# Seven inner products in place of one product, twice, in the second input phase of a pooling trunk; two operand sums stored instead of formed again; another form of the last rows' factor

## The chip, the core and the metric

The kernel runs on one core of a Trainium2 chip. The metric is the time of one execution in device microseconds (us). Before the change three runs gave 906.63, 906.72 and 906.90 us; the median is 906.72 us.

## The reference

One layer is computed (`DEPTH = 1`, so mixer 0 alone): a pooling mixer between two norms, over 4096 frames of 1024 channels.

```python
def trailing_mean(u, window):
    seq = u.shape[1]
    cs = jnp.cumsum(u.astype(jnp.float32), axis=1)
    lagged = jnp.pad(cs, ((0, 0), (window, 0), (0, 0)))[:, :seq]
    count = jnp.minimum(jnp.arange(1, seq + 1), window).astype(jnp.float32)
    return ((cs - lagged) / count[None, :, None]).astype(u.dtype)

def pool_mixer(h, in_w, group_w, group_b, scale, out_w):
    b, s, _ = h.shape
    u, gate = jnp.split(h @ in_w, 2, axis=-1)
    ug = u.reshape(b, s, POOL_GROUPS, POOL_GROUP_DIM)
    pooled = jnp.stack([trailing_mean(ug[:, :, g], w) for g, w in enumerate(POOL_WINDOWS)],
                       axis=2) - ug
    mixed = jnp.einsum('bsgc,gcd->bsgd', pooled, group_w) + group_b
    y = mixed.reshape(b, s, POOL_WIDTH) * scale * jax.nn.silu(gate)
    return y @ out_w

def reference(...):
    h = x
    h = h + pool_mixer(rms_norm(h, norm_w[0]), ...)
    return rms_norm(h, final_norm_w)
```

## The kernel before

**Products.** Every large matrix product is cut once into halves and done as seven products of the half size, in the form of Strassen and Winograd (P1 to P7, with sums S1 to S4 of the left operand's quarters and T1 to T4 of the right one's). Each fp32 operand is split into a high part (a copy, on ACT) and a low part (a subtraction, on DVE), both of type fp32r, and a product is three passes: high by high, high by low, low by high.

**Phases.** The list `steps` has 112 products: input phase a (four blocks of 1024 frames, seven products each; the weights with the group map folded in), input phase b (the same four blocks, the other half of the outputs), and the output phase o (eight blocks of 512 frames, seven products each). In phase b the order inside a block is P1, P2, P6, P7, P5, P4, P3. A product of phase a or b (`product_in`, line 711) is 48 matmuls of 512 columns: two halves of the inner dimension, four PSUM banks, two slices, three passes. Four of the output phase's products in a block are plain, too; P2 and P4 of most blocks are themselves done as seven inner products of a quarter of the size (`mm_inner`, line 826), of 6 matmuls with 256 columns each.

**PSUM.** There are eight banks. In the input phases banks 69 to 72 (by the names in the order below) are the set x, which P1, P2, P7 and P4 write, and 73 to 76 the set y, which P6, P5 and P3 write. After P1, its result is copied from x to y so that the others add to it. A product's result is taken out by `evict_in`: after P4 four DVE additions of one bank each, then a Silu on ACT over two tiles; after P3 four ACT copies. P1 of the next block starts on x straight behind P3, bank by bank.

**Operands.** Four tiles op_85 to op_88 hold two products' token operands (two tiles each). While a product runs, `split_halves` splits the next one's operand (`split`, line 216: ACT copy, then DVE subtraction), as soon as PE has released the tile. The operands of phase b are loaded from `sd`, where phase a stores them (`split_in`, line 656; the store is put on the ACT queue, on POOL's for block 0). S1 is formed anew in phase b by `form_in` at P5 (two DVE additions for a block), S4 by `form_s4` (two subtractions) in blocks 0 and 1; blocks 2 and 3 load a stored S4.

**What sets the order.** The loop at the end of the kernel runs step n: loads for steps ahead (`load_reach`), the operand two steps ahead (`form`), the split one step ahead, the pooling work that is due (`pool_due`), then the product and its eviction. `pool` (line 891) takes the results of P4 and P3, with running sums (`TENSOR_TENSOR_SCAN`), and stores rows for phase o; for phase b it also forms sums of them (`inner_sums`) and stores these to `sumd`. `make_wo` in steps b1 P5 and b2 P5 (b1 is block 1 of phase b) loads four tiles of the output weights, scales them on ACT, combines them on DVE and stores the results to `wod`. Engines work through their own instructions in order. Tiles come from two pools, st (11 tiles) and vt (8).

**The end.** For the last 256 rows `late_factor` (line 1163) forms 1/root by a reciprocal and one step of Newton's method, and `late_vector` applies it in two pieces of 256 columns.

Of the kernel before, what the change touches and what calls it, by code (L numbers as in the profile page):

```python
# [2 lines left out]

# [12 lines left out]
P = 128  # L16
D = 1024
# [14 lines left out]
S4_STORED = (2, 3)  # L32
# [7 lines left out]
class Slots:  # L40
# [41 lines left out]
    def retire(self):  # L82
        return self.free.popleft()[1]


@with_exitstack
def kernel(
# [51 lines left out]
    def new_st(i):  # L139
# [5 lines left out]
    vt = Slots(  # L145
        [mem.tile([P, 2 * (HIST + H)], F32, tag=f"vt{i}", name=f"vt{i}") for i in range(NV)]
    )
# [58 lines left out]
    def split(dst, src):  # L206
# [20 lines left out]
        for i in range(P1, P7 + 1)  # L227
# [4 lines left out]
            for i in (P1, P2, P7, P4, *((P3,) if b in S4_STORED else ()))  # L232
# [80 lines left out]
    def store_weights(dst, h, b11, b21, b12, b22):  # L313
        nc.sync.dma_start(out=dst[P1][h], in_=b11)
        nc.sync.dma_start(out=dst[P2][h], in_=b21)
        if P2 in firsts:
            inner_rights(P2, b21)
        for i, u in combine(b11, b21, b12, b22).items():
            nc.sync.dma_start(out=dst[i][h], in_=u)
            if i in firsts:  # L320
                inner_rights(i, u)
# [59 lines left out]
    def split_wb(i):  # L381
        for h in range(2):
# [7 lines left out]
            if i != P6:  # L390
                give(u)

    QW = H // 4

    def inner_rights(i, low):

        high = firsts.pop(i)
        more = take()
# [11 lines left out]
    firsts = {}  # L410

    def make_wo(h):
        if h:
            for i in INNER:
                firsts[i] = take()
                nc.sync.dma_start(out=firsts[i], in_=wod[i][0])
# [192 lines left out]
    def load_in(q, b, i):  # L609
# [11 lines left out]
        elif i == P3 and has_s4(q, b):  # L621
            s["12"] = load_saved(b, P3)

    def has_s4(q, b):
        return q == 1 and b in S4_STORED

    def form_in(q, b, i):
# [19 lines left out]
        elif i == P5:  # L647
# [6 lines left out]
    def split_in(q, b, i):  # L654
# [6 lines left out]
        if i == P6 and (q or b) and not has_s4(q, b):  # L661
            form_s4(b)
        if i == P2 and has_s4(q, b):
            for u in s.pop(key):
                give(u)
# [3 lines left out]
        elif i not in (P1, P2, P6) and not (i == P7 and swapped(q, b)):  # L669
            for u in s.pop(key):  # L670
                give(u)
        return t

# [30 lines left out]
    def product_in(i, t, sets, by_bank, between=None, behind=None):  # L704
# [17 lines left out]
        if between and 8 in between:  # L722
            between[8]()

# [166 lines left out]
    def pool(b, q, half, vs, sgs):  # L891
# [4 lines left out]
        for g in range(2):  # L896
# [44 lines left out]
            if win > 2:  # L941
                if first:
# [3 lines left out]
                    )  # L946
                nc.vector.scalar_tensor_tensor(
# [18 lines left out]
        if q:  # L966
            if 2 * b + 1 - half in sumd:
                inner_sums(2 * b + 1 - half, sgs)
            for sg in sgs:
                give(sg)  # L970
# [8 lines left out]
    def evict_in(b, q, i, sets):  # L979
# [26 lines left out]
        else:  # L1006
            ev["12"] = [take_v() for _ in range(2)]
            for c, u in enumerate(cells(ev["12"], HIST)):
                last = copy(halved(u), plain(ps[c]))
# [132 lines left out]
    def mean_part(ss, before):  # L1142
# [3 lines left out]
            out=ms, in0=ss, scalar1=1.0 / D, scalar2=before, op0=ALU.mult, op1=ALU.add  # L1146
# [10 lines left out]
    def early_half(half, j, n):  # L1157

        u = hs[NBO - 1][half, j][:, n]
        partial[half, j] = mean_part(square_part(halved(u)), EPS)  # L1160
        mul(u, u, fw[0][:, n])

    def late_factor(half, j, parts):
# [4 lines left out]
        tmp = column()  # L1168
        rs = column()
        behind = partial["added"]  # L1170
        scaled = column()
        nc.vector.tensor_scalar(
# [561 lines left out]
```

## Time and profile before

| | |
|---|---|
| median of three runs | 906.72 us (906.63 to 906.90) |
| profiled execution | 906.22 us, of which the span is 904.2 us |
| instructions | 11947 |
| ACT | 482.8 us busy, 53% of the span |
| POOL | 39.6 us busy, 4% |
| DMA | 200.66 MB, mean 222 GB/s |

The span is the stretch from the first to the last instruction of the profiled execution. A busy time is the time in which at least one instruction of an engine ran, and a matmul's end is modelled, so that neighbouring matmuls overlap in the record: how fast PE really goes is read from the starts of successive groups. In a group's row the second number behind the bar is the mean length of one instruction; instructions of one engine that follow each other start a little earlier than the first one's end. In square brackets stands how long an engine was idle before an instruction, and what ended that.

### The profile page before, as it was taken

The numbers are of one execution on the slowest core, as the hardware profiler recorded it, in microseconds if no ns is written. First come the engines' busy times: TensorE is split into PE (matmuls) and PEld (weight loads), VectorE is DVE, ScalarE is ACT, GpSimd is POOL, SyncE is SP. The second block draws the span as 40 slices with busy tenths as digits, with TensorE's granted clock in tenths as the row PEclk, the third lists the DMA queues.
The fourth block names the chain that finished last, engine by engine and source line by source line (L and its number), as shares of the span: only waits on it lengthen the run. The fifth ranks groups of instructions, "written<-read, shape, count | busy, mean of one in ns | idle before, by whom it ended". The sixth has DMA issues, their size and how long they took to land.

```text
span 904.2 us, 11947 instructions
## 1 busy us (share of the span) xinstructions
PE 895.7 (99%) x4446; PEld 789.8 (87%) x4446; DVE 767.4 (85%) x952; ACT 482.8 (53%) x794; POOL 39.6 (4%) x73
## 2 busy tenths in 40 slices
PE   9999999999999999999999999999999999999996
PEld 7888888888888888888888888888898998999996
DVE  5999993894998997497699499789999989889887
ACT  6979557447346555345355545654445535345354
POOL 0023102001100000000000000000001000000000
PEclk9999999999999999999999999999999999999999
DMA  9986966756866835116815776855875584584652
GB/s 349 408 318 162 347 212 209 253 187 237 324 211 233 278 117 186 47 47 220 315 69 201 288 281 222 295 181 193 278 251 196 195 308 151 176 292 148 212 186 94
DMA packets 73850, 200.66 MB, mean 222 GB/s; under 512 B 6784, under 2 KB 29696, under 8 KB 73792
## 3 DMA queue, kind: packets, MB, share of 16 engines
q1 hardware_dynamic: 66720, 176.54, 55.2%
q10 hardware_dynamic: 4752, 15.74, 4.6%
q0 software_dynamic: 2320, 7.62, 2.4%
q8 instruction: 35, 0.57, 0.3%
q14 instruction: 23, 0.19, 0.1%
HBM read 127.51 MB, written 72.36 MB: 221 GB/s over the span
## 4 chain that ended last, share of the span: by engine, by line
PE 97%; DVE 1%; DMA 0%; ACT 0%; issue 0%; DVEq 0%; ACTq 0%
PE bank L698 88%; PE bank L833 6%; PE bank L473 3%; DMA early<-in_wut 0%; DVE op L189 0%; DVE w L189 0%; DVE st L189 0%; PE bank L539 0%; ACT vt L1152 0%; DVE st L1232 0%; ACT vt L1193 0%; ACT vt L203 0%; ACT columns L1175 0%; DVE st L1204 0%; DVEq L1730 0%
## 5 line engine op out<-in xcount | busy, mean ns | idle before, releaser
L698 PE MATMUL bank<-op,w 128*128 128x512 f32 x2688 | 581.3, 379 | 0.1
L698 PEld LDWEIGHTS bank<-op,w 128*128 128x128 f32 x2688 | 507.6, 189 | 73.3 <-ACT early L203 0.6
L698 PE MATMUL bank<-w,op 128*128 128x512 f32 (+1 forms) x1068 | 232.2, 377 | 0.0
L698 PEld LDWEIGHTS bank<-w,op 128*128 128x128 f32 x1068 | 198.3, 189 | 26.9 <-issue 0.2
L189 DVE TENSOR_TENSOR op<-st,op 128x1024 fp32r<-128x1024 f32 x113 | 137.2, 1218 | 51.2 <-ACT op L203 51.0
L203 ACT ACTIVATE op<-st 128x1024 fp32r<-128x1024 f32 x113 | 118.4, 1052 | 95.1 <-PE bank L698 70.7
L203 ACT ACTIVATE op<-vt 128x1024 fp32r<-128x1024 f32 x65 | 67.6, 1052 | 48.0 <-PE bank L698 27.7
L189 DVE TENSOR_TENSOR op<-vt,op 128x1024 fp32r<-128x1024 f32 x65 | 78.6, 1215 | 7.3 <-ACT op L203 7.3
L203 ACT ACTIVATE vt<-bank 128x512 f32<-128x512 f32 x96 | 54.7, 592 | 51.4 <-PE bank L698 40.0
L203 ACT ACTIVATE bank<-bank 128x512 f32<-128x512 f32 (+1 forms) x72 | 36.5, 509 | 62.8 <-PE bank L698 32.1
L189 DVE TENSOR_TENSOR st<-st,st 128x1024 f32<-128x1024 f32 (+1 forms) x51 | 56.5, 1124 | 13.6 <-ACT st L294 9.3
L203 ACT ACTIVATE w<-st 128x1024 fp32r<-128x1024 f32 (+1 forms) x29 | 27.7, 964 | 27.0 <-PE bank L698 15.8
L1232 DVE TENSOR_TENSOR vt<-bank,vt 128x512 f32<-128x512 f32 x56 | 37.9, 680 | 3.0 <-PE bank L698 3.0
L189 DVE TENSOR_TENSOR st<-st,vt 128x1024 f32<-128x1024 f32 (+1 forms) x36 | 40.2, 1142 | 0.0
L189 DVE TENSOR_TENSOR vt<-bank,vt 128x512 f32<-128x512 f32 x50 | 33.2, 685 | 8.1 <-PE bank L698 8.1
L833 PE MATMUL bank<-w,op 128*128 128x256 f32 x288 | 39.9, 275 | 0.0
L189 DVE TENSOR_TENSOR w<-st,w 128x1024 fp32r<-128x1024 f32 (+1 forms) x29 | 31.9, 1107 | 8.8 <-ACT w L203 8.6
L833 PEld LDWEIGHTS bank<-w,op 128*128 128x128 f32 x288 | 37.8, 191 | 1.3
L925 DVE TENSOR_TENSOR_SCAN vt<-vt,bf 128x512 f32<-128x512 f32 x28 | 34.5, 1269 | 1.1 <-ACT vt L203 1.1
L1086 POOL TENSOR_SCALAR oms<-oss 128x2 f32<-128x2 f32 x14 | 7.4, 531 | 617.7 <-ACT st L1113 475.4
L203 ACT ACTIVATE st<-bank 128x512 f32<-128x512 f32 x34 | 20.0, 596 | 25.5 <-PE bank L698 18.5
L189 DVE TENSOR_TENSOR vt<-vt,vt 128x1024 f32<-128x1024 f32 (+1 forms) x28 | 32.8, 1175 | 0.5 <-DMA vt<-rd 0.5
(126 smaller groups left out, 676.1 us busy)
## 6 DMA issues: line engine op xcount, KB each, us to landing
st<-sd SPq DMA_DIRECT2D x31, 512.0 KB, 5.7
st<-in_x SPq DMA_DIRECT2D x30, 512.0 KB, 5.8
st<-in_xt SPq DMA_DIRECT2D x27, 512.0 KB, 7.8
vt<-in_x SPq DMA_DIRECT2D x27, 512.0 KB, 5.4
sd<-st ACTq DMA_DIRECT2D x25, 512.0 KB, 6.0
vt<-yd SPq DMA_DIRECT2D x18, 512.0 KB, 5.6
out<-vt SPq DMA_DIRECT2D x17, 512.0 KB, 3.2
yd<-vt SPq DMA_DIRECT2D x16, 512.0 KB, 2.8
```

Source lines behind the costliest of these rows:

```text
L189: made.append(nc.vector.tensor_tensor(out=dst, in0=a, in1=b, op=op))
L203: made.append(nc.scalar.activation(dst, src, func, **how))
L473: latest[0] = nc.tensor.matmul(ps2[kk][:, j * 256 : (j + 1) * 256], a[:, kk, 2 * j + t, :], maps if len(pairs) == 1 else woven(maps), star ...
L698: latest[0] = nc.tensor.matmul(ps, a, b, start=start and n == 0, stop=stop and n == 2, skip_group_check=True).ins
L833: latest[0] = nc.tensor.matmul(dst, a[k][x_], b[k][y_], start=start and k + n == 0, stop=k == 1 and n == 2, skip_group_check=True,).ins
L925: nc.vector.tensor_tensor_scan(s[:, j, at:end], v[:, j, at:end], v[:, j, at - win : end - win], sums_of[j] if sums_of else 0.0, ALU.add, A ...
L1086: nc.gpsimd.tensor_scalar(out=ms, in0=ss, scalar1=-0.5 / D, scalar2=-0.5 * EPS, op0=ALU.mult, op1=ALU.add)
L1232: partial["added"] = nc.vector.tensor_tensor(out=dst, in0=src, in1=dst, op=ALU.add).ins
```

## The change

`INNER_IN = (0, 1)` makes P3 of blocks b0 and b1 seven inner products (`product_inner`): each is 12 matmuls of 256 columns, 84 in all. The token side needs four more sums (`token_sums`, DVE) and four more splits of 512 columns; the weight side is prepared once, at b0 P6 (`keep_sums`). Three inner products use the banks x as working space, and partial results are copied from bank to bank on ACT. Twelve DVE additions of a quarter bank (`add_shared`) bring the shared parts into the result behind the ACT copies. Six tiles of st are lent to the new operands in b0 and b1 (three for the weights through both blocks, three for the tokens during each P3). `keep_sums` overwrites a quarter of the weights of P3, which is loaded and split again at b2 P2 for the two blocks that keep the plain P3.

`STORED` makes phase a store S1 (P5) for all four blocks and S4 (P3) for all four; phase b loads them. That is 12 more stores and 12 more loads of 512 KB, and phase b forms neither S1 nor S4. The tables of waits for `pool`, of the tiles kept free and of the reach of the loads get new values in phase b. `late_factor` replaces the Newton step, and the last `late_vector` is cut at 128 columns (pieces of 128 and 384) in place of 256. `inner_rights` loads its first tile itself, behind the stores of `make_wo`, where `make_wo` took it ahead of its own loads.

```diff
+INNER_IN = (0, 1)
+STORED = {3: (0, 1, 2, 3), 5: (0, 1, 2, 3)}
...
     def load_in(q, b, i):
...
-        elif i == P3 and has_s4(q, b):
-            s["12"] = load_saved(b, P3)
+        elif q and is_stored(i, b):
+            s["11" if i == P5 else "12"] = load_saved(b, i)
...
     def form_in(q, b, i):
...
-        elif i == P5:
+        elif i == P5 and not (q and is_stored(P5, b)):
             for h in range(2):
                 add(s["11"][h], s["2"][h], s["11"][h])
...
+    def token_sums(t, us):
+        b11, b12, b21, b22 = (
+            u.rearrange("p k (s a) -> p k s a", s=2)[:, :, :, n * P : (n + 1) * P]
+            for u in us for n in range(2)
+        )
...
+        sub(b11, b12, b11)
+        sub(b12, b22, b12)
+        sub(b22, b22, b11)
+        sub(b21, b21, b22)
...
+            split(dst, src)
...
+    def mm_inner_in(left, right, banks_, n, start):
+        a = inner_left_w[left]
+        for c in range(2):
+            for k in range(2):
+                for m, (x_, y_) in enumerate(((0, 0), (0, 1), (1, 0))):
...
+                        latest[0] = nc.tensor.matmul(
+                            quarter_bank(banks_[c], n), a[:, x_, k, c * P : (c + 1) * P],
+                            right[:, y_, k], ...)
...
+    def product_inner(t, sets):
+        r, tags = t
+        y, x = sets["y"], sets["x"]
+        in_turn[0] = None
+        mm_inner_in("A22", r["T4"], y[2:4], 0, False)
+        mm_inner_in("A11", r["B11"], x[2:4], 0, True)
+        for c in range(2):
+            copy(quarter_bank(x[c], 0), quarter_bank(x[2 + c], 0))
+        mm_inner_in("A12", r["B21"], y[0:2], 0, False)
+        mm_inner_in("S2", r["T2"], x[0:2], 0, False)
+        for c in range(2):
+            copy(quarter_bank(x[c], 1), quarter_bank(x[c], 0))
+        mm_inner_in("S4", r["B22"], y[0:2], 1, False)
+        mm_inner_in("S3", r["T3"], x[0:2], 1, False)
+        mm_inner_in("S1", r["T1"], x[2:4], 1, True)
+        for tag in tags:
+            restore(tag)
+
+    def add_shared(us, sets):
+        x = sets["x"]
...
+        for c in range(2):
+            into(c, 1, quarter_bank(x[c], 0))
+        for c in range(2):
+            for n in range(2):
+                latest_add = into(2 + c, n, quarter_bank(x[c], 1))
+        drained.append(latest_add)
+        for c in range(2):
+            into(c, 0, quarter_bank(x[2 + c], 0))
+            for m in range(2):
+                into(2 * m + c, 1, quarter_bank(x[2 + c], 1))
...
     def late_factor(half, j, parts):
...
-        partial["last"] = nc.scalar.activation(tmp, ss, AF.Sqrt, bias=before, scale=1.0 / D)
...
-        nc.vector.reciprocal(out=rs, in_=tmp)
-        nc.vector.scalar_tensor_tensor(
-            out=tmp, in0=rs, scalar=ms, in1=rs, op0=ALU.mult, op1=ALU.mult
-        )
-        nc.vector.scalar_tensor_tensor(
-            out=rs, in0=tmp, scalar=1.5, in1=rs, op0=ALU.add, op1=ALU.mult
-        )
+        partial["last"] = nc.scalar.activation(root, ss, AF.Sqrt, bias=before, scale=4.0 / D)
+        ms = mean_part(ss, before)
+        inverse = column()
+        nc.vector.reciprocal(out=inverse, in_=ms)
+        nc.vector.reciprocal(out=rs, in_=root)
+        nc.vector.scalar_tensor_tensor(
+            out=rs, in0=root, scalar=inverse, in1=rs, op0=ALU.mult, op1=ALU.add
+        )
...
-            late_vector(half, 1, n, factors[1], 2)
+            late_vector(half, 1, n, factors[1], H // 4)
...
     def pool_later(n):
-            wait = 0 if kind == "a" else 1 if b < NB - 1 else 2
+            wait = 0 if kind == "a" else (2, 1, 1, 2)[b]
...
-            wait = 1 if kind == "a" else 2 if b < NB - 1 else 5
+            wait = 1 if kind == "a" else (2, 3, 2, 5)[b]
...
-        return 3 if kind == "a" and i == P6 else 4 if kind == "o" else 3
+        return 2 if kind == "b" and b - 1 in INNER_IN and i in (P1, P2, P6) else 4 if kind == "o" else 3
...
+        if INNER_IN and kind == "b" and b == INNER_IN[0] and i == P6:
+            with tc.issue_after(latest_split[0]):
+                keep_sums(kept)
+        if INNER_IN and kind == "b" and b == INNER_IN[-1] and i == P3:
+            for tag in left_tags:
+                restore(tag)
```

Three places of the order show where the change sits. The first is PE at the end of b1. A row is a line of code, an operation, the tile it writes and the tiles it reads (stationary, for `product_in`, listed second), the columns, and how many alike follow each other. Before, P3 is eight groups of six, and P1 of b2 follows on bank_69:

```order
L698 MATMUL bank_73<-op_87,w_0_803 128x512 x6
L698 MATMUL bank_74<-op_87,w_0_803 128x512 x6
L698 MATMUL bank_75<-op_87,w_0_803 128x512 x6
L698 MATMUL bank_76<-op_87,w_0_803 128x512 x6
L698 MATMUL bank_73<-op_88,w_1_804 128x512 x6
L698 MATMUL bank_74<-op_88,w_1_804 128x512 x6
L698 MATMUL bank_75<-op_88,w_1_804 128x512 x6
L698 MATMUL bank_76<-op_88,w_1_804 128x512 x6
L698 MATMUL bank_69<-op_85,w_0_77 128x512 x6
```

And now, from the fourth group of six on (r_st are the lent tiles):

```order
L816 MATMUL bank_72<-op_87,w_0_817 128x256 x6
L816 MATMUL bank_73<-op_88,w_1_818 128x256 x6
L816 MATMUL bank_74<-op_88,w_1_818 128x256 x6
L816 MATMUL bank_69<-r_st_3431,r_st_2743 128x256 x6
L816 MATMUL bank_70<-r_st_3431,r_st_2743 128x256 x6
L816 MATMUL bank_73<-op_88,w_0_817 128x256 x6
L816 MATMUL bank_74<-op_88,w_0_817 128x256 x6
L816 MATMUL bank_69<-r_st_3434,r_st_2749 128x256 x6
L816 MATMUL bank_70<-r_st_3434,r_st_2749 128x256 x6
L816 MATMUL bank_71<-r_st_3437,r_st_2746 128x256 x6
L816 MATMUL bank_72<-r_st_3437,r_st_2746 128x256 x6
L783 MATMUL bank_69<-op_85,w_0_77 128x512 x6
```

P3 now writes banks 69 to 72, which P4 used just before and P1 of the next block needs straight behind.

The second place is DVE there, from P4's eviction on. Before, the eviction is followed by the pooling scans:

```order
L189 TENSOR_TENSOR vt_101<-bank_69,vt_101 128x512
L189 TENSOR_TENSOR vt_101<-bank_70,vt_101 128x512
L189 TENSOR_TENSOR st_90<-st_89,st_90 128x1024
L189 TENSOR_TENSOR vt_105<-bank_71,vt_105 128x512
L189 TENSOR_TENSOR vt_105<-bank_72,vt_105 128x512
L189 TENSOR_TENSOR op_86<-st_96,op_86 128x1024
L925 SCALAR_TENSOR_TENSOR vt_103<-vt_100,bf_1_2_0_3381 128x512
L925 SCALAR_TENSOR_TENSOR vt_103<-vt_100,bf_1_2_1_3384 128x512
L925 SCALAR_TENSOR_TENSOR vt_107<-vt_106,bf_1_3_0_3394 128x512
```

Now two scans stand ahead of the additions that free the banks (bf is a column that ACT computes):

```order
L215 TENSOR_TENSOR vt_106<-bank_71,vt_106 128x512
L215 TENSOR_TENSOR vt_106<-bank_72,vt_106 128x512
L215 TENSOR_TENSOR op_86<-st_95,op_86 128x1024
L1070 SCALAR_TENSOR_TENSOR vt_105<-vt_100,bf_1_2_0_3608 128x512
L1070 SCALAR_TENSOR_TENSOR vt_105<-vt_100,bf_1_2_1_3611 128x512
L215 TENSOR_TENSOR op_87<-st_92,op_87 128x1024
L848 TENSOR_TENSOR vt_101<-bank_69,vt_101 128x2x128
L848 TENSOR_TENSOR vt_103<-bank_69,vt_103 128x2x128
L848 TENSOR_TENSOR vt_101<-bank_70,vt_101 128x2x128
L848 TENSOR_TENSOR vt_103<-bank_69,vt_103 128x2x128
```

The additions on bank_69 come behind two scans and the low part of another operand, and wait for ACT's copies of P3's own banks.

The third place is DVE ahead of b2 P6, whose operand (the subtraction of two loaded tiles, then op_85) is now written into the tile that `inner_sums` has just stored:

```order
L1094 SCALAR_TENSOR_TENSOR vt_100<-vt_100,vt_102 128x2x512
L215 TENSOR_TENSOR w_0_817<-s_st_3588,w_0_817 128x2x256
L215 TENSOR_TENSOR vt_106<-vt_100,vt_106 128x1024
L215 TENSOR_TENSOR s_st_3038<-vt_107,vt_106 128x512
L215 TENSOR_TENSOR s_st_3038<-s_st_3038,vt_107 128x512
L215 TENSOR_TENSOR st_95<-vt_106,s_st_3038 128x512
L215 TENSOR_TENSOR s_st_3038<-vt_105,s_st_3589 128x1024
L215 TENSOR_TENSOR st_95<-vt_102,s_st_3590 128x1024
L215 TENSOR_TENSOR op_85<-s_st_3038,op_85 128x1024
```

Before, the same stretch read:

```order
L947 SCALAR_TENSOR_TENSOR vt_107<-vt_107,vt_106 128x2x512
L189 TENSOR_TENSOR st_95<-vt_101 128x512
L189 TENSOR_TENSOR vt_105<-vt_107,vt_105 128x1024
L189 TENSOR_TENSOR op_87<-st_99,op_87 128x1024
L189 TENSOR_TENSOR st_93<-vt_101,vt_105 128x512
L189 TENSOR_TENSOR st_93<-st_93,vt_101 128x512
L189 TENSOR_TENSOR op_88<-st_94,op_88 128x1024
L189 TENSOR_TENSOR st_95<-vt_105,st_93 128x512
L189 TENSOR_TENSOR st_93<-st_98,st_92 128x1024
L189 TENSOR_TENSOR st_96<-st_93,st_96 128x1024
L189 TENSOR_TENSOR op_85<-st_89,op_85 128x1024
```

The kind of work is the same; its place moved: behind P3's additions now, before them in the old order.

193 lines of the change are left out of this document (144 added, 49 removed).

## The prediction

> **What bounds the kernel now.** I read the page's busy times first, then its chain of waits, then PE's own waits.
>
> ```profile
> span 904.2 us, 11947 instructions
> PE 895.7 (99%) x4446; PEld 789.8 (87%) x4446; DVE 767.4 (85%) x952; ACT 482.8 (53%) x794; POOL 39.6 (4%) x73
> PE 97%; DVE 1%; DMA 0%; ACT 0%; issue 0%; DVEq 0%; ACTq 0%
> PE bank L1341 <- PEq L1719: 0.8, 1, 0.8
> PE bank L473 <- DMA early<-in_wut: 0.6, 1, 0.6
> ```
>
> PE is busy for 99% of the span and holds 97% of the chain that ended last. The last two rows are all its waits (total, times, longest): 1.4 us, both outside phase b. So an edit counts if it shortens PE's own work, makes PE wait, or sits behind the last matmul. DVE and ACT count only if they become late.
>
> Two groups of one line give phase b its place:
>
> ```profile
> L698 PE MATMUL bank<-op,w x2688: 379/379/483, 30.7 to 612.5; 128*128 128x512 f32 x192
> L698 PE MATMUL bank<-w,op x1068: 272/379/403, 612.7 to 896.9; 128*128 128x512 f32 x174, 128*128 128x256 f32 x4
> ```
>
> The first is all 56 products of both input phases (56 x 48 = 2688), the second the output phase. Phase b ends at 612.7. With no PE wait in it, it began 28 products earlier.
>
> **The price of a product.** The output phase already has both kinds of matmul behind each other; the second number of a row is its length, x12 and x6 its matmuls:
>
> ```profile
> 662.58 2.76 PE L698 MATMUL bank<-w,op 128*128 128x512 f32 x12
> 665.17 0.83 PE L833 MATMUL bank<-w,op 128*128 128x256 f32 x6
> ...
> 668.52 0.83 PE L833 MATMUL bank<-inner_T,op 128*128 128x256 f32 x6
> 669.19 1.03 PE L698 MATMUL bank<-w,op 128*128 128x512 f32 x4
> ```
>
> Ends are modelled, so I take starts. From 662.58 to 665.17, 12 matmuls of 512 columns take 2.59 us, 215.8 ns each. From 665.17 to 669.19 the six groups, 36 matmuls of 256 columns, take 4.02 us, 111.7 ns each. A plain P3 is 48 x 215.8 = 10.36 us; phase b thus starts at 612.7 - 28 x 10.36 = 322.6. Seven inner products are 84 x 111.7 = 9.38 us. Each replaced P3 saves 0.98 us of PE, and b0 and b1 together **1.96 us**. That is the ceiling of the main edit; an eighth of the columns goes (42 of 48 matmuls' worth), but the smaller matmul costs 3.8 ns more than half of the large one.
>
> A price below the row's is excluded by no row but has none for it; one above it has this:
>
> ```profile
> L833 PEld LDWEIGHTS bank<-w,op 128*128 128x128 f32 x288 | 37.8, 191 | 1.3
> ```
>
> Here 288 weight loads keep the loader busy for 37.8 us, 131 ns each, more than a matmul of 256 columns. In the rows above they are hidden all the same (111.7 ns from start to start). I take 111.7; if a load set the pace with the new operands, an inner P3 would be 84 x 131 = 11.0 us, 0.6 more than the plain one. That is rival R.
>
> The Trainium skill ("TensorE: Matmul & The Clock Gate", section "Back-to-back issue gap") speaks against the change: it gives about 81 ns for a matmul with its load at 128 columns and 131 ns at 512 in a sustained stream, so that narrow ones are dear per column. On a line between the two, my estimate is some 98 ns at 256: 8.2 us for an inner product against 6.3 for a plain one, a loss of 1.9 each, 3.8 us in all. This trace's 215.8 and 111.7 agree with neither figure, nor with their ratio.
>
> **What DVE and ACT get.** Busy time of PE, PEld, DVE and ACT (count in brackets), in blocks b0, b1 and b2 of phase b:
>
> ```profile
> 322.40:395.00 72.60, 72.60 (x338) 63.58 (x337) 53.84 (x59) 34.36 (x46) 0.00 (x0) 1.00 0.30 102
> 395.00:467.50 72.50, 72.50 (x338) 63.48 (x337) 54.33 (x54) 34.98 (x68) 0.00 (x0) 1.00 0.49 181
> 467.50:540.10 72.60, 72.60 (x338) 63.58 (x337) 56.61 (x60) 36.53 (x69) 0.00 (x0) 1.00 0.69 254
> ```
>
> DVE is idle for 18.8 us in b0 and 18.2 us in b1. Its prices, from rows of several instructions or from start to start:
>
> ```profile
> 438.08 2.35 DVE L189 TENSOR_TENSOR st<-st,st 128x1024 f32<-128x1024 f32 x2
> 454.53 1.28 DVE L189 TENSOR_TENSOR vt<-bank,vt 128x512 f32<-128x512 f32 x2
> 456.86 1.31 DVE L189 TENSOR_TENSOR vt<-bank,vt 128x512 f32<-128x512 f32 x2
> 460.25 3.63 DVE L925 TENSOR_TENSOR_SCAN vt<-vt,bf 128x512 f32<-128x512 f32 x3 [0.41 <-ACT vt L203]
> 881.63 1.42 DVE L841 TENSOR_TENSOR st<-bank,st 128x256 f32<-128x256 f32 x4 [0.98 <-PE bank L833]
> L203 ACT ACTIVATE bank<-bank 128x256 f32<-128x256 f32 x24 | 8.8, 368 | 30.7 <-PE bank L833 15.5 <-DVE vt L1232 12.2 <-DVE st L1232 3.0
> ```
>
> That is 1.14 us for 1024 columns (2.35 less the overlap of a tenth), 0.60 for 512, 0.355 for a quarter bank, 1.2 for a scan, and on ACT 0.37 for a copy from bank to bank. Removed from DVE: S1 in four blocks (8 additions) and S4 in two (4 subtractions), 12 x 1.14 = 13.7 us. Added: `keep_sums` 8 x 0.60 = 4.8; for each inner P3 four sums and four low parts, 8 x 0.60, and 12 quarter additions, 4.3, so 9.1 each and 18.2 for two; the restored quarter of the weights 0.6. That is 23.6, **net +9.9 us**, 9.3 of it in b0 and 4.5 in b1, less in the others. Both fit into the idle time, so the totals cost nothing and only the hand-overs can; without that slack PE would wait for up to 9.3 us in b0 and 4.5 in b1. On ACT a P3 adds four copies from bank to bank (1.5 us) and four high parts of 512 columns, against some 37 us idle in a block.
>
> **Hand-overs at P3.** I walk b1 with t = 0 at P4's first matmul; PE's groups by the prices above. P4 ends at 10.36, and the seven inner products follow in steps of 1.34 until P1 of b2 wants bank_69 at 19.74. The engines' side starts from these rows:
>
> ```profile
> 447.12 1.06 ACT L203 ACTIVATE op<-st 128x1024 fp32r<-128x1024 f32 x1 [4.12 <-PE bank L698]
> 457.53 1.06 ACT L203 ACTIVATE op<-st 128x1024 fp32r<-128x1024 f32 x1 [0.63 <-PE bank L698]
> ```
>
> They are the splits released by the ends of P5 and P4 (10.4 us apart, P4 from 446.95). The first new operand, T4's low part, is ready at about 6.3 and needed at 10.36. P4's last bank leaves by DVE at 11.3 (the pair at 456.86 ends at 458.17, 11.2 after 446.95) and the inner product A11 B11 needs it at 12.37. The two bank copies behind A11 B11 end at 13.3 and 14.1, needed at 14.38 and 15.05; the second pair at 16.4 and 16.9, needed at 17.06 and 17.73. The last quarter addition on bank_69 ends at 19.45, P1 needs it at 19.74. That **0.3 us** is the smallest margin. It counts on DVE having done the two scans and the low part of op_87, 3.5 us, between the eviction at 11.3 and the first addition at about 17; in b0 it is 0.65 us. A stall here is bounded by one late quarter addition behind a scan, 0.36 + 1.2 = 1.6 us, and below by nothing. I take nothing.
>
> **Hand-overs of data.** `pool` for b0's P3 now comes one product later, and on SP two of the loads of `make_wo` in b1 stand behind its two `sumd` stores. Before:
>
> ```profile
> 419.55 0.33 SPq L279 DMA_DIRECT2D st<-in_out_w  x1
> 423.89 1.33 ACT L294 ACTIVATE st<-st,colt 128x512 f32<-128x512 f32 x2 [6.31 <-DMA st<-in_out_w]
> 434.54 2.49 DVE L189 TENSOR_TENSOR st<-st,st 128x1024 f32<-128x1024 f32 x2 [4.23 <-ACT st L294]
> st<-in_xt SPq DMA_DIRECT2D x27, 512.0 KB, 7.8
> ```
>
> A load landed 4.3 us after its issue (419.55 to 423.89), then two scalings of 0.6, then DVE, which had waited 4.23 us for them. Queued behind that wait on DVE are the low parts of P3's operands and the evictions of P5. A product later, the chain ends about 1.2 us before these are due, and P3's front bears 1.5 us more: a stall comes only from 2.7 us on. A load of 7.8 us, the slowest median for 512 KB here, is 3.5 late and stalls 0.8; one whose tile also waits for a slow store stalls longer (rival C). I take nothing, since 4.3 is the landing at this very place.
>
> The operand of b2 P6 is formed in a tile that `sumd` must have left. The same wait before:
>
> ```profile
> 472.68 2.05 SPq L885 DMA_DIRECT2D sumd<-st  x2
> 475.48 2.48 DVE L189 TENSOR_TENSOR st<-st,st 128x1024 f32<-128x1024 f32 x2 [1.10 <-DMA sumd<-st]
> 477.99 1.23 DVE L189 TENSOR_TENSOR op<-st,op 128x1024 fp32r<-128x1024 f32 x1
> DMA to landing us min/median/max: 2.6/4.1/7.5
> ```
>
> The store landed 2.8 us after its issue (472.68 to 475.48). Now the operand would be ready 19.3 us into b2 and is needed at 20.9. That bears a store of 4.4 us; the slowest of all `sumd` transfers, 7.5 us, would cost 3.1. I take nothing; ends 0 and 3.1. The other added loads and stores (24 x 512 KB) pass where DMA works at 0.30 and 0.49 of its time in b0 and b1; in phase a tiles come back some us later, with 3.4 us in hand at the tightest place I found (P1 of a's b1). DMA is hidden there by the two products' lead of the splits.
>
> **The end.** The last rows' factor:
>
> ```profile
> 898.52 0.29 ACT L1175 ACTIVATE columns<-columns 128x1 f32<-128x1 f32 x1
> 898.85 0.16 DVE L1181 RECIPROCAL columns<-columns 128x1 f32<-128x1 f32 x1
> 899.04 0.22 DVE L1182 SCALAR_TENSOR_TENSOR columns<-columns 128x1 f32<-128x1 f32 x1
> 899.30 0.16 DVE L1185 SCALAR_TENSOR_TENSOR columns<-columns 128x1 f32<-128x1 f32 x1
> 899.49 0.88 DVE L1204 SCALAR_TENSOR_TENSOR st<-st,columns,st 128x256 f32<-128x256 f32 x2
> ```
>
> Root, reciprocal, two steps, product. The reciprocal of the mean fits under the root, and one step goes: 899.49 - 899.30 = **0.19 us**. The other cut of the last piece (128 and 384 columns) is the same work; its second store is half as large again, 0.1 us or so either way, which I leave out.
>
> **Sum.** The profiled execution took 906.22 us (span 904.2, 2.0 around it): 906.22 - 1.96 - 0.19 = 904.07. The median of the runs is 0.50 above that execution, so against 906.72 it is **904.6**.
>
> **Rivals.**
> A, the forecast: the whole gain, no new wait, 904.2 to 905.0 (the end's piece, and a few tenths of bank_69).
> B: one short wait takes the gain's place: bank_69 late at P1 (to 1.6 us), or the `sumd` store ahead of b2 P6 (to 3.1 us). 905.0 to 907.7. For it: margins of 0.3 and 1.6 us found by a walk with errors of their own; against it: the landings at these places, 2.8 and 4.3 us, are short.
> C, slower: `make_wo` in b1. Its third tile must be stored before it is loaded; a store of 7.5 instead of 4.1 us and a load of 7.8 instead of 4.3 make the chain 6.9 us late, 2.7 are borne, P3's front stalls 4.2 us: 908.8. It decides from 4.7 us on, where 2.0 of stall takes the gain. For it: SP's queue holds both stores ahead; against it: both slow at once, at a DMA share of 0.49.
> R: weight loads set the pace of the new matmuls: 906.72 + 2 x 0.6 - 0.19 = 907.7. Against it stand the 36 matmuls at 111.7. By the skill's two figures it would be 906.72 + 3.8 - 0.2 = 910.3, an estimate.
>
> **How the numbers follow.** A 0.56, B 0.21, C 0.20, R 0.03. A measurement of this kernel tells 0.2%, 1.8 us, from no change: faster is below 904.91, slower above 908.53. Of A a chance of 0.04 lies between 904.91 and 905.0. Faster 0.52; same 0.04 + 0.21 + 0.03 = 0.28; slower C, 0.20. The range runs from A with 0.3 more at the end and 0.4 of scatter, 903.9, over B to 908.0, and leaves out C's own value.
>
> **What would show it.** Right: in b0 and b1 the matmuls of 256 columns start 0.67 us apart in sixes, P3 lasts 9.4 us, phase b ends at 610.7 by the profile, and PE waits for nothing in it. For B, PE waits on DVE for a bank at the first matmul of b1 or b2, or on the low part of op_85 at b2 P6 with DVE idle for a `sumd` store. For C, DVE idles on ACT's scaling in b1 P5 and PE waits at P3's front. For R, sixes more than 0.7 us apart. At the end, the product after the reciprocal comes one step of 0.19 us sooner. The forecast is wrong if PE waits anywhere in phase b, phase a included, where I judged the later tiles to cost nothing.

## The result

The changed kernel takes 910.41 us (median of 6 runs, 908.79 to 911.81) against 906.55 us (906.32 to 906.90) in the same runs: a ratio of 1.0042, interval 1.0032 to 1.0052. It is 0.4% **slower**; the forecast was 904.6, and its range ended at 908.0.

The page of the profiled execution (911.81 us, the slowest of the six, of which the span is 910.0) begins:

```profile
span 910.0 us, 12205 instructions
PE 897.5 (99%) x4518; PEld 792.0 (87%) x4518; DVE 776.0 (85%) x985; ACT 489.0 (54%) x815; POOL 40.3 (4%) x77
PE 80%; DVE 11%; DMA 5%; issue 2%; ACT 1%; DVEq 0%; SPq 0%; ACTq 0%
```

PE is still busy for 99%, but of the chain that ended last it holds 80%, not 97%: 11% has gone to DVE and 5% to DMA. PE's own waits (total, times, longest):

```profile
PE bank L783 <- DVE op L215: 4.1, 2, 2.2
PE bank L1493 <- PEq L1894: 0.8, 1, 0.8
PE bank L783 <- DVE vt L848: 0.5, 1, 0.5
PE bank L497 <- DMA early<-in_wut: 0.2, 1, 0.2
PE bank L816 <- ACT bank L229: 0.2, 1, 0.2
PE bank L816 <- DVE vt L215: 0.2, 1, 0.2
```

The first row is new and the largest: two waits for the low part of an operand. The rows with L816 lie in b1's P3, the one with L848 at the first matmul behind it. The waits add up to less than the loss: a modelled matmul end reaches into each of them, and slower matmuls are no wait. So I count from start to start: the time from a product's first matmul to the next product's, for all 56 products of the input phases. Those that changed (us):

```
product        before   changed
a1 P7           10.36     10.55
a3 P1           10.36     12.88
b0 P6           10.36     14.22
b0 P3           10.36      9.38
b1 P3           10.36     11.23
b2 P1           10.36     10.46
```

The sum is +6.56 us, and the output phase begins 6.5 us later by the profile (619.2 against 612.7). From there to the end of the span it is 290.8 us against 291.5. So the inner product costs what was forecast (9.38), and three places give back far more: **the two largest, a3 P1 and b0 P6 with 6.4 us together, lie outside the products that were changed.** This is the profiled execution; the median of the runs lost 3.9 us, and how much less each place cost in the other runs is not known.

**Where DVE is late.** DVE in phase a's block 2 of the changed kernel (start, length, operation, and in brackets how long it was idle and what ended that):

```profile
221.97 1.23 DVE L215 TENSOR_TENSOR st<-st,st 128x1024 f32<-128x1024 f32 x1 [2.43 <-DMA st<-wvd]
...
230.44 1.22 DVE L215 TENSOR_TENSOR st<-vt,st 128x1024 f32<-128x1024 f32 x1 [3.94 <-DMA st<-wvd]
...
239.86 2.36 DVE L215 TENSOR_TENSOR vt<-vt,vt 128x1024 f32<-128x1024 f32 x2 [4.08 <-DMA vt<-rd]
...
249.08 1.22 DVE L215 TENSOR_TENSOR op<-vt,op 128x1024 fp32r<-128x1024 f32 x1
...
252.86 1.22 DVE L215 TENSOR_TENSOR op<-vt,op 128x1024 fp32r<-128x1024 f32 x1
```

And the same stretch before the change:

```profile
222.94 1.23 DVE L189 TENSOR_TENSOR st<-vt,st 128x1024 f32<-128x1024 f32 x1 [4.76 <-DMA st<-wvd]
...
232.34 2.36 DVE L189 TENSOR_TENSOR vt<-vt,vt 128x1024 f32<-128x1024 f32 x2 [0.46 <-DMA vt<-rd]
...
241.56 1.21 DVE L189 TENSOR_TENSOR op<-vt,op 128x1024 fp32r<-128x1024 f32 x1
...
245.34 1.22 DVE L189 TENSOR_TENSOR op<-vt,op 128x1024 fp32r<-128x1024 f32 x1
```

The second subtraction that waits for a load from `wvd` comes at 230.44 in place of 222.94, 7.5 us late, and the pair after it as late (239.86 against 232.34). The pair needs a load from `rd` that POOL issues only behind that subtraction; in the changed kernel, and before:

```profile
232.07 0.59 POOL L584 DMA_DIRECT2D vt<-rd  x1 [6.76 <-DVE st L215]
```

```profile
224.57 0.57 POOL L560 DMA_DIRECT2D vt<-rd  x1 [7.20 <-DVE st L189]
```

The two low parts at the end of DVE's rows are the operand of a3 P1, which begins at 250.2: before, both were ready by 246.6; now the second is ready at 254.1, and PE, which stopped after six matmuls, goes on there. The loads from `wvd` are those of `save_t3` (L372), which subtracts weights and stores the result to `t3d`. SP's queue in the changed kernel, and before:

```profile
206.95 4.00 SPq L618 DMA_DIRECT2D vt<-in_xt  x2
213.09 4.26 SPq L372 DMA_DIRECT2D st<-wvd  x2
...
223.22 0.38 SPq L372 DMA_DIRECT2D st<-wvd  x1
```

```profile
208.06 0.33 SPq L346 DMA_DIRECT2D st<-wvd  x1
210.50 0.33 SPq L594 DMA_DIRECT2D vt<-in_xt  x1
213.74 4.79 SPq L346 DMA_DIRECT2D st<-wvd  x2
```

The first load into st is issued 5.0 us later, and the last one 5 us later too (223.22; before, the second of the last pair went out at 218.2); that one then takes 7.1 us to land in place of 4.7, which makes 7.5 of the 5. The tiles of the first two loads in the order of the program are st_96 and st_97, the two that held block 2's S1. Before, S1 was only split; now it is stored too, by ACT:

```profile
208.99 0.33 ACTq L609 DMA_DIRECT2D sd<-st  x1
...
211.81 0.33 ACTq L609 DMA_DIRECT2D sd<-st  x1
```

Both tiles are free only when these have landed; everything behind them on SP waits. SP's waits from 205 to 225 us (total, times, longest) have this row, which they do not have before:

```profile
SPq L372 <- DMA sd<-st: 5.6, 2, 3.6
```

**Why it is still late 100 us on.** DVE's busy time (third pair of numbers) in the changed kernel:

```profile
260.00:320.00 60.00, 60.00 (x280) 52.54 (x279) 53.38 (x58) 30.39 (x44) 0.00 (x0) 1.00 0.75 257
320.00:348.00 28.00, 26.35 (x123) 22.73 (x121) 28.00 (x30) 16.94 (x25) 0.00 (x0) 1.00 0.59 212
```

Its 6.6 us of pauses in the first 60 are no reserve: they are waits for three more loads, 2.22 us up to 288.82 and these:

```profile
297.10 1.42 DVE L389 SCALAR_TENSOR_TENSOR st<-st,colt,vt 128x512 f32<-128x512 f32 x2 [3.08 <-DMA vt<-t3d]
303.58 1.23 DVE L215 TENSOR_TENSOR vt<-vt,st 128x1024 f32<-128x1024 f32 x1 [1.28 <-DMA vt<-wvd]
```

Before, the wait for the second load from `t3d` ended at 289.16, so DVE is still 7.9 us late here. What makes these loads land late was not followed. From 303.58 DVE has no pause until 348. P6's operand is late in b0, and PE's loader stops for 2.3 us. Then something is added that no wait shows:

```profile
348.25 1.95 PEld L783 LDWEIGHTS bank<-op,w 128*128 128x128 f32 x7 [2.31 <-DVE op L215]
```

Two stretches of 2 us, before and after that wait, in the columns of the table above:

```profile
344.00:346.00 2.00, 2.00 (x11) 1.70 (x10) 2.00 (x4) 2.00 (x4) 0.00 (x0) 1.00 0.21 84
350.00:352.00 2.00, 2.00 (x6) 1.55 (x5) 2.00 (x3) 0.29 (x1) 0.00 (x0) 0.50 0.91 277
```

In both PE is busy for all of 2 us each, with 11 matmuls and then with 6: the number after POOL's is the granted clock, 1.00 and 0.50. P6 took 14.22 us, 3.86 more; the profile's record has the clock at a half for 3.41 us, which costs 1.7 of them.

### The profile page after: what moved, and what is told of

Same layout as the page of the kernel before. It is cut to its first block, busy times and chain, and to the rows that moved or that the text cites. A ratio compares the mean times of both kernels' runs of the same rounds, so it can differ in the third digit from the quotient of the medians.

```text
span 910.0 us, 12205 instructions
## 1 busy us (share of the span) xinstructions
PE 897.5 (99%) x4518; PEld 792.0 (87%) x4518; DVE 776.0 (85%) x985; ACT 489.0 (54%) x815; POOL 40.3 (4%) x77
## 4 chain that ended last, share of the span: by engine, by line
PE 80%; DVE 11%; DMA 5%; issue 2%; ACT 1%; DVEq 0%; SPq 0%; ACTq 0%
PE bank L783 70%; PE bank L972 6%; PE bank L497 3%; DVE vt L215 2%; DVE st L215 2%; DVE op L215 2%; DMA st<-wvd 1%; DVE vt L1070 1%; DVE w L215 1%; DVE vt L1094 1%; DMA vt<-rd 1%; PE bank L816 1%; DMA wod<-st 1%; DVE st L1102 1%; DVE vt L848 1%
## 5 line engine op out<-in xcount | busy, mean ns | idle before, releaser
L783 PE MATMUL bank<-op,w 128*128 128x512 f32 x2592 | 563.5, 380 | 4.8 <-DVE op L215 4.1
L783 PEld LDWEIGHTS bank<-op,w 128*128 128x128 f32 x2592 | 490.2, 189 | 76.9 <-DVE op L215 5.6
L229 ACT ACTIVATE op<-st 128x1024 fp32r<-128x1024 f32 x71 | 73.6, 1040 | 54.1 <-PE bank L783 26.5
L215 DVE TENSOR_TENSOR op<-st,op 128x1024 fp32r<-128x1024 f32 x71 | 84.9, 1202 | 19.6 <-ACT op L229 19.3
L229 ACT ACTIVATE vt<-bank 128x512 f32<-128x512 f32 x90 | 50.5, 589 | 31.8 <-PE bank L783 18.9
L229 ACT ACTIVATE op<-s_st 128x1024 fp32r<-128x1024 f32 x41 | 43.1, 1051 | 29.5 <-PE bank L783 21.7
L215 DVE TENSOR_TENSOR op<-s_st,op 128x1024 fp32r<-128x1024 f32 x41 | 49.8, 1216 | 1.2 <-ACT op L229 1.2
L215 DVE TENSOR_TENSOR st<-st,vt 128x1024 f32<-128x1024 f32 (+1 forms) x29 | 32.3, 1144 | 0.7 <-DMA vt<-rd 0.7
L229 ACT ACTIVATE st<-st 128x1024 f32<-128x1024 f32 x25 | 26.4, 1055 | 9.7 <-DVE st L215 7.8
L215 DVE TENSOR_TENSOR vt<-vt 128x1024 f32<-128x1024 f32 (+2 forms) x28 | 31.4, 1141 | 0.0
```

The source lines that it names most:

```text
L215: made.append(nc.vector.tensor_tensor(out=dst, in0=a, in1=b, op=op))
L229: made.append(nc.scalar.activation(dst, src, func, **how))
L783: latest[0] = nc.tensor.matmul(ps, a, b, start=start and n == 0, stop=stop and n == 2, skip_group_check=True).ins
```

## The experiments

Medians are of 4 to 11 runs; each ratio is against runs of the kernel before on the same chip.

**Three parts taken apart.** First the new factor alone, in the kernel before:

```diff
-        nc.vector.scalar_tensor_tensor(out=tmp, in0=rs, scalar=ms, in1=rs, ...)
-        nc.vector.scalar_tensor_tensor(out=rs, in0=tmp, scalar=1.5, in1=rs, ...)
+        nc.vector.reciprocal(out=inverse, in_=ms)
+        nc.vector.scalar_tensor_tensor(out=rs, in0=root, scalar=inverse, in1=rs, ...)
...
-            late_vector(half, 1, n, factors[1], 2)
+            late_vector(half, 1, n, factors[1], H // 4)
```

> The kernel before with the new late factor and the cut of the last piece at 128 columns alone. If the changed kernel's output phase is 0.7 us shorter because of this edit, the time is about 0.7 us under that of before (906.5 to 905.8). If the edit is worth only the one column step of the prediction, 0.19 us, it is 906.3. If the 0.7 us come from elsewhere, no difference.

906.32 against 906.33 us: 0.9998 (0.9989 to 1.0007), nothing. The step is saved all the same; in this kernel's DVE rows the last product starts at 899.29, 0.20 us before the 899.49 of the kernel before:

```profile
899.04 0.22 DVE L1175 SCALAR_TENSOR_TENSOR columns<-columns 128x1 f32<-128x1 f32 x1
899.29 0.88 DVE L1194 SCALAR_TENSOR_TENSOR st<-st,columns,st 128x128 f32<-128x128 f32 x2
```

Its larger last store, in the list of DMA issues at the end (size, us to landing),

```profile
out<-st SPq DMA_DIRECT2D x1, 192.0 KB, 2.8
```

lands after 2.8 us, where 128 KB took 2.4; the span is 904.3 against 904.2. This edit alone does not make the 0.7 us between the output phase's start and the end. They lie behind PE's last matmul, from which the end is 6.7 us away in the changed kernel, 7.3 before and 7.4 here; in the changed kernel the last store of 192 KB landed after 2.4 us, and what the rest is was not found.

Then the stores without inner products:

```diff
-INNER_IN = (0, 1)
+INNER_IN = ()
```

> The changed kernel without inner products (P3 of all blocks plain), S1 and S4 still stored for all blocks. Theory A, the added stores of phase a hold tiles and make DVE late: P1 of a's block 3 still takes about 12.9 us and b0's P6 about 14, and the time is about 911 to 912. Theory B, the sums of the inner products load DVE in b0: both take 10.36 us, and the time is 906 or less.

909.67 us, 1.0036 (1.0024 to 1.0049). Without a single inner product a3 P1 takes 11.13 us, b0 P6 12.38, and b3 P2 11.19. Theory A holds in kind; the sizes are smaller, and the forecast of 911 to 912 missed.

**Which store.** I first took the two stores at 208.99 and 211.81 for block 1's. They are block 2's, as the order of the program shows once each store is followed to its tile, so the next two runs moved the wrong ones:

```diff
-        t = split_halves(s[key], None if q or later else sd[b].get(i), b == 0)
+        t = split_halves(..., True if b == 0 else 1 if (b, i) == (1, P5) else False)   # 1: POOL's queue
```

> The changed kernel with one edit: block 1's two stores of S1 in phase a are issued by POOL, not by ACT. Theory A1, the lateness is that of these two stores' issue (208.99 and 211.81 us, behind ACT's squares), which holds st_96 and st_97 from the loads for t3: P1 of a's block 3 and b0's P6 fall back to 10.36 us and the time to about 904. Theory A2, the traffic of all added stores slows the loads, whichever queue issues them: both stay long, about 910.

908.95 us, 1.0031 (1.0020 to 1.0042); a3 P1 11.59, b0 P6 11.67, b1 P3 10.91. Neither theory's number.

```diff
-INNER_IN = (0, 1)
-STORED = {3: (0, 1, 2, 3), 5: (0, 1, 2, 3)}
+INNER_IN = (0,)
+STORED = {3: (0, 1, 2, 3), 5: (0, 2, 3)}
```

> The changed kernel with inner products in b0 alone, and S1 of block 1 not stored but formed again in phase b. Theory A1: phase a as before the change, b0's P6 10.36 us, b0's P3 9.38, b1's P3 10.36: 906.5 - 1.0 - 0.2 to 0.7 for the end = 904.8 to 905.3. Theory B (DVE's added sums in b0 are what makes b0's P6 late): P6 14 us, time about 908 to 909.

911.40 us, 1.0051 (1.0037 to 1.0064); a3 P1 13.13, b0 P6 11.40, b0 P3 9.38, b1 P7 11.48, b3 P2 11.48. With block 1's S1 not stored, a3 P1 is as late as ever: a miss for "block 1". The right stores then; on POOL's queue they are also no longer held behind the last eviction, as ACT's stores are (`tc.issue_after(evicted[0])`):

```diff
-        t = split_halves(s[key], None if q or later else sd[b].get(i), b == 0)
+        t = split_halves(..., True if b == 0 else 1 if (b, i) == (2, P5) else False)   # 1: POOL's queue
```

> The changed kernel with block 2's two stores of S1 in phase a issued by POOL in place of ACT (they were the ones at 208.99 and 211.81 us that held st_96 and st_97). Theory A1, these two stores' late issue: a's block 3 P1 and b0's P6 fall to 10.36 us, together 6.4 us less, and the time to about 904 to 906.5, where only b1's P3 (11.2 us) still waits. Theory A2, the traffic of the added stores: P1 of a's block 3 stays near 12 us and the time at 909 to 910.

**906.29 us**, 0.9997 (0.9988 to 1.0005): a3 P1 10.36, b0 P6 10.36, 6.4 us back in the profile and 4.1 by the medians, with every store and every byte still there. POOL issues the two stores earlier, SP's loads follow, and DVE's pair is at 236.50:

```profile
206.58 0.54 POOL L609 DMA_DIRECT2D sd<-st  x1 [38.81 <-DVE st L215]
207.71 0.53 POOL L609 DMA_DIRECT2D sd<-st  x1 [0.60 <-DVE st L215]
211.56 0.33 SPq L372 DMA_DIRECT2D st<-wvd  x1
236.50 2.36 DVE L215 TENSOR_TENSOR vt<-vt,vt 128x1024 f32<-128x1024 f32 x2 [3.18 <-DMA vt<-rd]
```

The start of that pair and the length of a3 P1 go together over the kernels:

```
                      pair starts   a3 P1
before                  232.34      10.36
e5_s1_b2_by_pool        236.50      10.36
e2_stores_only          238.10      11.13
e3_s1_by_pool           239.00      11.59
changed                 239.86      12.88
e4_inner_b0             240.02      13.13
```

Up to some 237 the lateness is covered; from there PE pays about 1 us for each (the rest of the scatter is PE's own start, 30.5 to 31.1). Among the late ones the start differs with the load from `rd`: the pair begins 6.8 us after its issue in e2_stores_only, 7.8 in the changed kernel. Leaving block 2's S1 unstored instead:

```diff
-STORED = {3: (0, 1, 2, 3), 5: (0, 1, 2, 3)}
+STORED = {3: (0, 1, 2, 3), 5: (0, 1, 3)}
```

> The changed kernel without storing S1 of block 2 (phase b forms it there again, as before the change). Theory A1: as with the stores by POOL, P1 of a's block 3 10.36 us, b0's P6 10.36 us, 904 to 906.5. Theory A2 (all other added stores are still there): P1 of a's block 3 about 12 us, 909.

a3 P1 and b0 P6 are 10.36 here as well, so the cause is confirmed a second way; but the time is 912.84 us, 1.0078 (1.0063 to 1.0094), because b2 P6 now takes 12.37 and b3 P2 12.80, and PE waits another 2.0 us in the output phase. The forecast of 904 to 906.5 missed. Ahead of b2 P6's operand DVE waits 3.43 us for a load from `sd` (to 489.26); why forming S1 again brings that was not traced.

**What is left: b1's P3.** In e5_s1_b2_by_pool it takes 11.42 us, 2.04 more than b0's. PE's loader there (start, length, operation, and its waits in brackets):

```profile
456.63 1.52 PEld L816 LDWEIGHTS bank<-op,w 128*128 128x128 f32 x12
458.69 2.75 PEld L816 LDWEIGHTS bank<-op,w 128*128 128x128 f32 x24 [0.53 <-DVE vt L215]
461.84 1.53 PEld L816 LDWEIGHTS bank<-r_st,r_st 128*128 128x128 f32 x12 [0.40 <-ACT bank L229]
...
468.27 6.77 PEld L783 LDWEIGHTS bank<-op,w 128*128 128x128 f32 x32 [0.70 <-DVE vt L848]
```

Three waits: P4's banks taken out late, a bank copy late, and at P1 of b2 the quarter additions. DVE's rows of the same kernel show where the first comes from:

```profile
438.14 1.22 DVE L215 TENSOR_TENSOR st<-st,st 128x1024 f32<-128x1024 f32 x1 [3.84 <-ACT st L320]
...
455.61 1.22 DVE L215 TENSOR_TENSOR op<-s_st,op 128x1024 fp32r<-128x1024 f32 x1 [0.25 <-ACT op L229]
456.75 2.48 DVE L215 TENSOR_TENSOR vt<-bank,vt 128x512 f32<-128x512 f32 x4
...
463.31 2.46 DVE L1070 TENSOR_TENSOR_SCAN vt<-vt,bf 128x512 f32<-128x512 f32 x2 [1.98 <-ACT vt L229]
465.69 1.20 DVE L215 TENSOR_TENSOR op<-st,op 128x1024 fp32r<-128x1024 f32 x1
466.80 4.06 DVE L848 TENSOR_TENSOR vt<-bank,vt 128x256 f32<-128x256 f32 x12
```

`make_wo`'s first combination waits until 438.14; from there to the four additions on P4's banks (456.75) DVE pauses twice for 0.25 us. They begin when P4 is done, where they could have followed it bank by bank. Two attempts on `make_wo`, two products earlier and with less work:

```diff
-            if kind == "b" and b in (1, 2) and i == P5:
+            if kind == "b" and (b, i) in ((1, P6), (2, P5)):
```

> As the run with block 2's S1 by POOL, and make_wo of b1 two products earlier (with P6, not P5). Theory C (make_wo's loads behind the sumd stores make DVE late at b1's P3): b1's P3 falls from 11.2 to about 9.4 us, 1.8 us less time than the run without this. Rival (DVE has no slack there, whenever make_wo comes): P3 stays at 11.

908.73 us, 1.0025 (1.0014 to 1.0036): b1 P3 13.70, longer, not 9.4. By the words above the rival has it; but this edit gave tiles another order, DVE waited 4.1 us more inside `make_wo`, and the granted clock fell again. It decides little about b1. It does show that b0's P6 is only just covered in e5_s1_b2_by_pool: with the same two stores on POOL and a3 P1 at 10.36, it takes 11.51 here and 11.86 in e9_scans_later below. In both, DVE's last wait for a load from `wvd` ends later (299.79 and 300.41; in e5_s1_b2_by_pool its last wait of this kind, for `t3d`, ends at 293.40). So the two stores are not all that can make b0's P6 late.

```diff
+        if not less:                    # less: make_wo of b1
             sub(b12, b22, b12)
             add(b11, b12, b11)
             sub(b21, b21, b11)
```

> As the run with block 2's S1 by POOL, with three of the four 1024-column subtractions and additions of make_wo in b1 left out (3.4 us of DVE; the first halves of the weights for P6, P7 and P4 of the output phase are then wrong). Theory: DVE comes out of make_wo's wait late and works without a pause until P4's banks are taken out; with 3.4 us less b1's P3 takes 9.4 to 9.6 us, time about 904.5. Rival: the waits of P3 come from the order of DVE and ACT inside P3 itself; P3 stays above 10.5.

**905.16 us**, 0.9985 (0.9976 to 0.9994), b1 P3 9.96, not quite the 9.4 to 9.6 expected, in a kernel that leaves three operations out and so computes part of the result wrongly: the first two waits are gone, and only the one at P1 of b2 is left. So it is the amount of DVE's work there, not the order inside P3, that makes P4's banks late. The last wait should be the scans':

```diff
-            wait = 0 if kind == "a" else (2, 1, 1, 2)[b]
+            wait = 0 if kind == "a" else (2, 2, 1, 2)[b]
```

> As the run with block 2's S1 by POOL (b1's P3 11.42 us), and the pooling of b1's P4 one product later, so that its two scans no longer stand ahead of the quarter additions. If the scans make the last wait (0.7 us at P1 of b2), b1's P3 falls by 0.7 to about 10.7, with the first two waits (0.5 and 0.4 us) left, and the time to about 905.6. If the scans are not the cause, P3 stays at 11.4.

b1 P3 takes 10.12, 1.3 us less where 0.7 were expected (PE also came to it 1.1 us later than in e5_s1_b2_by_pool, so not all of it need be the scans'); but the time is 915.79 us, 1.0102 (1.0088 to 1.0115), since b0 P6 took 11.86, b2 P3 12.04 and b3 P2 18.13. With the P3 results pooled sooner as well:

```diff
-            wait = 0 if kind == "a" else (2, 1, 1, 2)[b]
+            wait = 0 if kind == "a" else (2, 2, 1, 2)[b]
...
-            wait = 1 if kind == "a" else (2, 3, 2, 5)[b]
+            wait = 1 if kind == "a" else (2, 2, 2, 5)[b]
```

> As the run with the scans of b1's P4 later, and b0's P3 and b1's P3 pooled after two products, not three (as before the change). If the wait of make_wo's loads behind the sumd stores (a product later because of the three) starts DVE's lateness, b1's P3 falls below 10 us and the time to about 904.7 to 905. If not, P3 stays at 10.7.

915.41 us, 1.0100 (1.0084 to 1.0115); b1 P3 10.48, b3 P2 13.61, b3 P7 16.83. The wait of three products is not what makes b1 late; with PE no later at P3 than in e5_s1_b2_by_pool, 0.9 us less than there is about what the scans' wait was. One more with inner products in b0 alone:

```diff
-INNER_IN = (0, 1)
+INNER_IN = (0,)
```

> As the run with block 2's S1 by POOL, with inner products in b0 alone. If b1's waits belong to the inner P3: b1's P3 10.36 us, b0's P3 9.38, the time about 905.5, 1 us under before. If b1's make_wo is late without it as well, b1's P3 is over 10.5 us.

b1 P3 is 10.36, so `make_wo` alone does not stall a plain P3; but the time is 913.93 us, 1.0081 (1.0068 to 1.0094): b3 P2 15.45, b3 P7 14.29. What makes b3 late in these three (the low parts of operands, with the clock at a half after it) I did not trace back.

**A version to beat both** would keep DVE's slack in b1. POOL is idle in phase b, so it got `make_wo`'s four operations of b1:

```diff
-        sub(b12, b22, b12)
+        both(b12, b22, b12, ALU.subtract)     # nc.gpsimd for b1, nc.vector otherwise; so all four
```

> As the run with block 2's S1 by POOL, with the four 1024-column additions and subtractions of make_wo in b1 done by POOL, which is idle in phase b. If POOL takes them without slowing DVE, b1's P3 is 9.9 to 10.0 us as with three of them left out, and the time 905.0 to 905.4, under both kernels. If POOL is so slow that SP's stores of wod hold up the loads behind them, b2's first products wait and the time is above 906.5.

910.44 us, 1.0052 (1.0038 to 1.0066); b1 P4 12.57, b1 P3 13.58. POOL's rows, and DVE's beside them:

```profile
438.09 5.70 POOL L329 TENSOR_TENSOR st<-st,st 128x1024 f32<-128x1024 f32 x2 [197.79 <-ACT st L320]
443.87 3.23 POOL L329 TENSOR_TENSOR s_st<-st,st 128x1024 f32<-128x1024 f32 x1
438.99 2.56 DVE L215 TENSOR_TENSOR op<-s_st,op 128x1024 fp32r<-128x1024 f32 x1 [4.98 <-ACT op L229]
441.88 2.99 DVE L215 TENSOR_TENSOR op<-s_st,op 128x1024 fp32r<-128x1024 f32 x1 [0.34 <-ACT op L229]
444.79 3.38 DVE L215 TENSOR_TENSOR op<-vt,op 128x1024 fp32r<-128x1024 f32 x1
```

DVE's low parts, 1.22 us elsewhere, take 2.56 to 3.38 while POOL works, 5.3 us more for the three, against four operations of 1.14 us taken off DVE: nothing was gained. The time is above 906.5, as the second expectation had it, but PE waits at b1's P4 and P3, not at b2's first products. No kernel here that computes everything beats the one before by what can be measured; e5_s1_b2_by_pool equals it.

## Why the prediction was wrong

**Right.** The price of an inner product: b0's P3 takes 9.38 us, as worked out, in all kernels that have it but one (9.53 in e8_inner_b0_pool). Rival R falls with it. So do, for these matmuls (111.7 and 215.8 ns from start to start), the 81 and 131 ns of the Trainium skill ("TensorE: Matmul & The Clock Gate", section "Back-to-back issue gap"). DVE's added sums did not make b0 late: e2_stores_only has none of them and a b0 P6 of 12.38, and in e5_s1_b2_by_pool, with all of them, b0 runs at 10.36 and 9.38. The operand of b2 P6 behind the `sumd` store cost nothing. The column step saves 0.20 us where 0.19 were forecast.

**The step that failed: the added stores of phase a.** The prediction put them at nothing, "in phase a tiles come back some us later, with 3.4 us in hand at the tightest place I found (P1 of a's b1)". The tiles do come back about 5 us later, but the place was wrong: the two of block 2's S1 are next taken by `save_t3`, whose loads DVE waits for in order, and there DVE came 7.5 us late, where the operand of a3 P1 bears some 5 (232.34 to 237 in the table). It cost 2.5 us at a3 P1; the lateness went on to b0 P6, which lost 3.9, 1.7 of them to the clock. Both losses are gone in e5_s1_b2_by_pool and e6_s1_b2_not_stored; that b0's P6 can lose 1.15 to 1.5 us without them (e7_make_wo_early, e9_scans_later) stays open. I had followed who waits for the added loads and stores, and not who takes the tiles they hold, on a queue where every later load stands behind that one.

**A covered lateness was taken for a free one.** "DMA is hidden there by the two products' lead of the splits" holds up to some 237; behind that DVE's only long pauses are waits for loads that are late themselves, and from 303.58 to 348 it has none, so what is late stays late.

**The clock.** The half clock after b0 P6's wait, 1.7 us, was not in any rival.

**Rival B, right in part.** It named bank_69 at P1 of b2, and the loader does wait there, for 0.5 to 0.7 us. The larger part came earlier, inside P3, where the walk saw a margin. The walk of b1 had P4's last bank free 11.3 us after P4's start, needed at 12.37. In the changed kernel P4 starts at 452.45, and DVE's four additions run

```profile
462.54 2.48 DVE L215 TENSOR_TENSOR vt<-bank,vt 128x512 f32<-128x512 f32 x4
```

to 465.02, which is 12.6: 1.3 late, and the two copies and the quarter additions follow. P3 took 1.85 us more than its price (11.23 against 9.38), where B's bound for bank_69 alone was 1.6.

**Rival C did not happen as priced, but prepares B.** `make_wo`'s late loads did not stop P3's front. DVE left that wait without slack, and 3.4 us less work removed the first two waits (e10_less_combine).

**The end.** The step of 0.19 us came, but e1_factor_only cannot tell it from nothing (its interval is some 0.8 us to either side), and there the larger last store takes 2.8 us to land in place of 2.4.

Without the two stores' cost the time is 906.3 (e5_s1_b2_by_pool), with b1's waits of 2.0 us in it, and 905.2 with most of those gone as well (e10_less_combine, which leaves work out). The forecast's 904.6 is near that, but no run shows it.

## What to carry to other kernels

A store that is added "behind" other work holds its tile until it lands: follow that tile to its next owner, then the queue on which that owner's load stands, then the engine that waits for it in order; and ask how far behind it the engine's first pause is that is not itself a wait for something late. Where PE is at 97% of the chain, a lost microsecond on another engine shows up in products that the edit never touched, so compare product by product before forming a theory. Issuing two stores some 2 to 4 us earlier, from an idle queue, was worth more here (4.1 us by the medians) than the arithmetic that the edit saves (1.96).

## What the runs showed of the hardware

**The clock falls after a short wait, not always.** A wait of 2.63 us of PE's loader (ended at 254.13) left the granted clock at 1.00; one of 2.31 us (ended at 348.25) was followed by 3.41 us at 0.50. The Trainium skill ("TensorE: Matmul & The Clock Gate", section "Part 1: The HAM clock gate (the "warmup" mystery)") names the same 3.41 us as the length of a free-running window, and idle windows of about that length as the cause; the length agrees, but here less than that of idling was enough once. Other kernels are as mixed: a wait of PE of 2.98 us (ended at 553.14, e11_both_pools) left the clock at 1.00, one of 1.79 us (ended at 462.16, e7_make_wo_early) was followed by 0.50. What decides it is open. The clock alone does not make the spread of the changed kernel's runs (908.79 to 911.81): the run of 911.30 us has a mean granted clock of 0.999, the one of 911.81 has 0.997.

**POOL and DVE do not add up** on additions whose inputs both lie in SBUF: 1.22 us became 2.56 to 3.38. An eviction beside them, with one input in a bank, kept its pace (two in 1.27 us at 448.10). The Trainium skill ("SBUF — State Buffer", section "SBUF: two separate sides") says that such a DVE operation and one of POOL lock the same port pair for a whole instruction each; both numbers agree with it.
